# A mixer stage whose small products stand a step later, and first modulation weights in the buffers of the main inputs

## The chip, the cores and the metric

One core of a Trainium2 chip runs the whole program in one launch. The metric is the time of one execution in device microseconds; the time before is the median of three runs. TensorE (PE) multiplies, VectorE (DVE), ScalarE (ACT) and GpSimd (POOL) do the rest, and SyncE (SP) issues nearly all transfers.

## What is computed

Two transformer-like blocks follow each other on 512 tokens of width 1024; 256 context tokens go through the first block's first layer too. All is fp32. Only the first block is touched by the change. Each of its two layers is, cut to what matters:

```python
mx = split(silu(c) @ w_ada[l] + b_ada[l], 6)          # modulation, main stream
mc = split(silu(c_ctx) @ w_ada[l] + b_ada[l], 6)      # modulation, context
hx = modulate(rmsnorm(x, g), mx[0], mx[1]); hc = modulate(rmsnorm(ctx, g), mc[0], mc[1])
zx = hx @ w_in; zc = hc @ w_in
# mLSTM, 4 heads of 128, forward and backward: the context's final state starts the main stream
# gates -> running sums and maxima; scores q k^T * exp(...); states sum(w * k v^T); normalise per head
# plus a Fourier mix over 256 channels and a 31-tap depthwise convolution over 256 channels
out = concat([mlstm, fourier, conv]) @ w_out
x = x + mx[2] * rmsnorm(out); then a squared-ReLU MLP with its own modulation
```

## The kernel before

Large products run as three fp32r passes: each operand is split into a high part (a cast on ACT) and a low part (a subtraction on DVE), and lines 317 to 319 multiply high by high and the two mixed pairs. Weights come in tiles of 128x1024 (0.52 MB) through three staging buffers `st`, and `wload` (line 273 on) casts and subtracts them into four `whi` and four `wlo` buffers. Small products, those of attention and states, are plain fp32, in two passes each.

The program is written as Python code whose scheduler orders each engine's instructions by its own estimates, so the order on an engine is not the order of the source. What is hand-made is a set of side threads. A product group of the large kind (`gemm_f`, `gemm_t`) ends with `self.step(rate)`: three steps for the 512 main tokens, one for the 256 context tokens. A step resumes the next of up to three side generators to its next `yield`. So a `yield` places what follows it behind at least one more product group. The threads of a layer's `mixers` are: one per stream for the gates (`gate_thread`, line 718), one per head and stream (`head_thread` in `head`, line 847), the convolution, the Fourier mix, and a `tail` that turns and splits the finished heads. `finish` (line 306) runs out the remaining steps when the in-projections are done: there a step has no product group beside it. The finished channels lie in the tiles that held the layer's input (`new_h`), so the turning of heads waits for the last in-projection product.

In a head, `ktrans` turns the keys on PE and copies them on ACT; `kstate` scales them on ACT (line 836), a slot each, and multiplies each by the values (line 837) right behind; the sum goes into the state. The context's heads make the state, the main stream's heads use it. `short_conv` (lines 805 to 808) makes the queries and keys, `gate_thread` the gate rows, and its transposes follow two yields after their transfer.

The program opens with the first modulation. `ada_now` (line 430) loads 16 tiles of 0.52 MB through the three `st` buffers and multiplies each by the two condition vectors (line 442) on PE; columns 2 and 3 of the weight blocks first, then 0 and 1. The two context tiles are loaded and normalised meanwhile (`prenorm_a`), then modulated and split (`prenorm_b`, lines 514, 511, 313). The main inputs are loaded behind the modulation (`first_load`), get their position codes added, half on DVE, half on POOL (line 1252), and the values' weights (`win_v`) are loaded by the first `wload` of `mixers`.

Of the kernel before, what the change touches and what calls it, by code (L numbers as in the profile page):

```python
# [9 lines left out]
F32 = mybir.dt.float32  # L10
# [3 lines left out]
AF = mybir.ActivationFunctionType  # L14
OP = mybir.AluOpType

P = 128
D = 1024
T = 512
TC = 256  # L20
KT = D // P
# [9 lines left out]
NST = 3  # L31
# [195 lines left out]
class Net:  # L227
# [202 lines left out]
    def ada_now(self, w, nbs, mods):  # L430

        nc = self.nc
        n = len(mods)
        bias = self.par1[0]
        for nb in nbs:
            ps = self.psum("mm")
            for c in range(4):
                with self.tc.high_priority():
                    st = self.ws.tile([P, 1024], F32, tag="st", name=self.nm("st"), bufs=NST)
                    nc.sync.dma_start(st, w[2 * nb + c // 2][:, 1024 * (c % 2):1024 * (c % 2) + 1024])  # L440
                for k in range(2):
                    nc.tensor.matmul(ps[:n], self.cvec[:, 2 * c + k:8 * n:8], st[:, 512 * k:512 * k + 512],
                                     start=c + k == 0, stop=c + k == 4)
            row = self.slot()[:n]
            nc.vector.tensor_copy(row, ps[:n])
            ps = self.psum("s")
            for f in range(4):
                self.transpose(ps[:, n * f:n * f + n], row[:, P * f:P * f + P])
            e = slice(4 * nb, 4 * nb + 4)
            for m, mod in enumerate(mods):  # L450
                nc.vector.tensor_add(mod[:, e], ps[:, m:4 * n:n], bias[:, e])
# [273 lines left out]
    def gate_thread(self, g, li, fz, bg, t, prior, key):  # L725
        nc = self.nc
# [26 lines left out]
        nt = t // P  # L753
# [14 lines left out]
        w = li  # L768
# [7 lines left out]
        nc.sync.dma_start(dr[:, :t], M)  # L776
        yield
        yield
        ut = self.small("ut_k" if key else "ut_x", [P, 4, 2, R], bufs=1)
        wt = self.small("wt_k" if key else "wt_x", [P, 4, R], bufs=1)  # L780
        for i in range(nt):
            ps = self.psum("s")
# [10 lines left out]
        ps = self.psum("s")  # L793
# [34 lines left out]
            next(after, None)  # L828
        return v

    def kstate(self, hd, d, g, kt, v, tiles, pv):

        r = hd + 32 * d
        for n, i in enumerate(tiles):
            ks = self.slot((P, P))
            self.nc.scalar.activation(ks, kt[:, P * i:P * i + P], AF.Copy, scale=g["w"][:, i, r:r + 1])
            self.nc.tensor.matmul(pv, ks, v[:, i, hd], start=n == 0, stop=n == len(tiles) - 1)

    def ktrans(self, k, nt):
        ps = self.psum("s")  # L840
# [6 lines left out]
    def head_thread(self, hd, q, k, v, g, t, prior, new, out):  # L847


        nc = self.nc  # L850
        nt = t // P
        while not g:
            yield
        kt = self.ktrans(k, nt)
        if new is not None:
            pv = self.psum("pv")
            for d in range(2):
                self.kstate(hd, d, g, kt, v, range(nt), pv[:, 130 * d:130 * d + 130])
            nc.vector.tensor_copy(new["c"][:, hd], pv[:, :260].rearrange("p (d n) -> p d n", n=130))
            new[hd] = True  # L860
            if out is None:
                return
            yield
# [9 lines left out]
        for c in range(nch):  # L873
# [5 lines left out]
            for d in range(2):  # L879
# [19 lines left out]
                n = 0  # L899
# [8 lines left out]
        if prior is not None:  # L908
            while hd not in prior:
                yield  # L910
            states = prior["c"]
            for d in range(2):
                r = hd + 32 * d
                x = self.slot()
                for c in range(nch):
                    e = slice(256 * c, 256 * c + 256)
                    ref = g["mref"][:, 0 if (c == 0) == (d == 0) else 1, r:r + 1]
                    nc.scalar.activation(x[:, e], negm[d][:, e], AF.Exp, bias=ref)
                nc.vector.tensor_mul(x, x, q)
                qs.append(x)  # L920
            st1 = self.slot((P, 2, 130))
            pv = self.psum("pv")
            for d in range(2):
                self.kstate(hd, d, g, kt, v, (0, 1) if d == 0 else (2, 3), pv[:, 130 * d:130 * d + 130])
            for d in range(2):
                r = hd + 32 * d
                nc.vector.scalar_tensor_tensor(st1[:, d], states[:, hd, d], g["mref"][:, 2, r:r + 1],
                                               pv[:, 130 * d:130 * d + 130], op0=OP.mult, op1=OP.add)
            yield
# [179 lines left out]
    def mixers(self, l, streams, after=iter(())):  # L1109
# [6 lines left out]
        for m in streams:  # L1116
# [4 lines left out]
                whole.append(m)  # L1121
            if key:
                ctx["c"] = self.hp.tile([P, 4, 2, 130], F32, tag="cstate", name=self.nm("cstate"))
        ws = [self.wload(a["win_v"][l, c]) for c in range(2)]
        for m in streams:
            m["v"] = self.values(ws, m["h"], m["t"], "vc" if m["key"] else "vx", after)
        w = self.wload(a["win_g"][l, 0], 1024)
# [73 lines left out]
    def first_block(self):  # L1201
# [34 lines left out]
        with self.tc.high_priority():  # L1236
            xc = [self.prenorm_a(self.first_load(sc, i)[0]) for i in range(2)]
        self.ada_now(a["w_ada"], (2, 3, 0, 1), mods[0])
        xx = [self.first_load(sx, i) for i in range(4)]
        hc = self.new_h(TC, "c")  # L1240
        g = gs(0, 1, 0, "g_pre_mix")()
# [6 lines left out]
        def rest():  # L1248
            for i in range(4):
                xh, pos = xx[i]  # L1250
                for j in range(2):
                    (nc.gpsimd if j else nc.vector).tensor_add(xh[j], xh[j], pos[j])
                self.prenorm_b(self.prenorm_a(xh), i, *g, hx)
                yield
            with self.tc.issue_after(self.last_load):
# [667 lines left out]
```

## Time and profile before

| | |
|---|---|
| median of three runs | 2852.14 us (2851.42, 2852.14, 2858.28) |
| profiled execution | 2859.91 us, span of its trace 2858.1 us |
| PE busy | 2718.5 us, 95% of the span |
| DVE, ACT, POOL busy | 1686.4, 1097.8, 301.7 us |
| PE's mean granted clock | 0.973 of full |
| moved by DMA | 312.85 MB, 109 GB/s over the span |

The busy time of an engine is the union of its instructions' spans. A wait is put down to the producer that came last. The small products leave two records each in the trace, the transposes one. In the layers of the first block the mixers lie at about 60 to 380 us and 1040 to 1260 us; the opening lies ahead of them.

### The profile page before, as it was taken

The numbers are of one execution on the slowest core, as the hardware profiler recorded it, in microseconds if no ns is written. First come the engines' busy times: TensorE is split into PE (matmuls) and PEld (weight loads), VectorE is DVE, ScalarE is ACT, GpSimd is POOL, SyncE is SP. The second block draws the span as 40 slices with busy tenths as digits, with TensorE's granted clock in tenths as the row PEclk, the third lists the DMA queues.
The fourth block names the chain that finished last, engine by engine and source line by source line (L and its number), as shares of the span: only waits on it lengthen the run. The fifth ranks groups of instructions, "written<-read, shape, count | busy, mean of one in ns | idle before, by whom it ended". The sixth has DMA issues, their size and how long they took to land. (4 is left out here: it accounts for less than half of the span.)

```text
span 2858.1 us, 36796 instructions
## 1 busy us (share of the span) xinstructions
PE 2718.5 (95%) x13940; PEld 2197.9 (77%) x13940; DVE 1686.4 (59%) x3469; ACT 1097.8 (38%) x2032; POOL 301.7 (11%) x452
## 2 busy tenths in 40 slices
PE   6999998999999988998999999999999999999998
PEld 2888888888788866877888877776788777766887
DVE  3587856567734679965334467666433566674334
ACT  2543545322222364544323353445222444353222
POOL 2042001000000013201000010010012100101011
PEclk8989999999999999998999999999999999999999
DMA  7323323445612463443223332221132422111223
GB/s 271 105 84 105 106 85 108 151 132 182 230 61 67 163 200 111 133 156 132 96 81 108 106 129 89 74 75 38 46 102 89 147 76 88 53 60 41 92 89 118
DMA packets 101281, 312.85 MB, mean 109 GB/s; under 512 B 11504, under 2 KB 15368, under 8 KB 101104
## 3 DMA queue, kind: packets, MB, share of 16 engines
q1 hardware_dynamic: 100544, 309.64, 33.1%
q8 instruction: 109, 1.79, 0.3%
q0 software_dynamic: 560, 0.86, 0.1%
q14 instruction: 68, 0.56, 0.1%
HBM read 293.43 MB, written 17.03 MB: 109 GB/s over the span
## 5 line engine op out<-in xcount | busy, mean ns | idle before, releaser
L317 PE MATMUL mm<-xhi,whi 128*128 128x512 f32 (+2 forms) x1520 | 595.3, 392 | 15.8 <-DVE sl L1400 7.0
L285 DVE TENSOR_TENSOR wlo<-st,whi 128x1024 fp32r<-128x1024 f32 x352 | 441.5, 1260 | 284.6 <-ACT whi L284 279.0
L284 ACT CAST whi<-st 128x1024 fp32r<-128x1024 f32 x352 | 369.0, 1050 | 593.0 <-PE mm L318 283.4
L318 PE MATMUL mm<-xlo,whi 128*128 128x512 f32 (+2 forms) x1520 | 589.9, 388 | 0.4 <-DVE xlo L313 0.2
L319 PE MATMUL mm<-xhi,wlo 128*128 128x512 f32 (+2 forms) x1520 | 590.2, 388 | 0.0
L317 PEld LDWEIGHTS mm<-xhi,whi 128*128 128x128 f32 (+1 forms) x1520 | 289.9, 191 | 73.4 <-DVE sl L1400 7.8
L319 PEld LDWEIGHTS mm<-xhi,wlo 128*128 128x128 f32 (+1 forms) x1520 | 289.9, 191 | 56.9
L318 PEld LDWEIGHTS mm<-xlo,whi 128*128 128x128 f32 (+1 forms) x1520 | 289.7, 191 | 56.6 <-issue 1.5
L317 PE MATMUL mm<-whi,sl 128*128 128x512 f32 x640 | 250.9, 392 | 3.2 <-DVE sl L696 1.3
L319 PE MATMUL mm<-whi,sl 128*128 128x512 f32 x640 | 250.1, 391 | 1.0 <-DVE sl L313 1.0
L318 PE MATMUL mm<-wlo,sl 128*128 128x512 f32 x640 | 250.5, 391 | 0.5 <-DVE wlo L285 0.2
L317 PE MATMUL mm<-whi,xhi 128*128 128x512 f32 x576 | 229.6, 400 | 4.5 <-ACT xhi L313 4.5
L318 PE MATMUL mm<-wlo,xhi 128*128 128x512 f32 x576 | 228.8, 397 | 0.2
L319 PE MATMUL mm<-whi,xlo 128*128 128x512 f32 x576 | 227.8, 396 | 0.6 <-DVE xlo L313 0.4
L352 PE MATMUL s<-ident,sl 128*128 128x128 f32 (+2 forms) x756 | 123.5, 284 | 63.4 <-ACT sl L511 15.2
L352 PEld LDWEIGHTS s<-ident,sl 128*128 128x128 f32 (+2 forms) x756 | 87.6, 144 | 115.3 <-issue 34.4
L383 DVE CUSTOM_DVE_ANT_0 sa<-sa,crow 128x1024 f32<-128x1024 f32 x112 | 137.0, 1225 | 40.5 <-DMA sa<-in_w_ada 27.4
L317 PEld LDWEIGHTS mm<-whi,sl 128*128 128x128 f32 x640 | 120.6, 188 | 30.6 <-DVE sl L696 1.9
L319 PEld LDWEIGHTS mm<-whi,sl 128*128 128x128 f32 x640 | 120.6, 188 | 26.7 <-DVE sl L313 1.8
L318 PEld LDWEIGHTS mm<-wlo,sl 128*128 128x128 f32 x640 | 120.6, 188 | 26.6 <-DVE wlo L285 2.1
L313 ACT CAST sl<-sl 128x512 fp32r<-128x512 f32 (+2 forms) x144 | 70.6, 500 | 171.9 <-DVE sl L650 129.4
L317 PE MATMUL mm<-chi,whi 128*128 128x256 f32 (+1 forms) x448 | 134.6, 301 | 1.1 <-ACT chi L313 1.1
(372 smaller groups left out, 4372.4 us busy)
## 6 DMA issues: line engine op xcount, KB each, us to landing
st<-in_w_mlp SPq DMA_DIRECT2D x128, 512.0 KB
st<-in_win_a SPq DMA_DIRECT2D x116, 512.0 KB
sa<-in_w_ada SPq DMA_DIRECT2D x80, 512.0 KB
sa<-in_ada SPq DMA_DIRECT2D x48, 512.0 KB
st<-in_win_b SPq DMA_DIRECT2D x40, 512.0 KB
st<-in_w_out SPq DMA_DIRECT2D x32, 512.0 KB
xres<-sl SPq DMA_DIRECT2D x48, 256.0 KB
sl<-xres SPq DMA_DIRECT2D x48, 256.0 KB
```

Source lines behind the costliest of these rows:

```text
L284: nc.scalar.copy(hi, st)
L285: nc.vector.tensor_sub(lo, st, hi.bitcast(F32))
L313: return self.nc.scalar.copy(hi, src), self.nc.vector.tensor_sub(lo, src, hi.bitcast(F32))
L317: mm(ps, l[0], r[0], start=first, stop=False)
L318: mm(ps, l[0], r[1], start=False, stop=False)
L319: self.last_mm = mm(ps, l[1], r[0], start=False, stop=last).ins
L352: self.nc.tensor.transpose(out, src, self.ident[:p, :p])
L383: nc.vector.tensor_tensor_reduce(x, st[:, e], row[:, e], 1.0, 0.0, op0=OP.mult, op1=OP.add, accum_out=part[:, m, f, h:h + 1])
```

## The change

It has three parts. The first modulation's weights go into the two tiles that later hold the main stream's split input (`xhi` and `xlo`, tags of the pool `hx`): four loads to a tile, alternating, with all eight products of a block behind them in the source, and the value weights are then loaded at once behind the last of these loads, ahead of the main inputs. The four additions of position codes that POOL did go to DVE. And the threads have more yields: one in the gates ahead of their transposes; one at the start of a head; one in context heads behind the key transposes; and one inside `kstate` between the scaled copies, which now go into one slot, and the products with the values.

```diff
         for b, nb in enumerate(nbs):
             ps = self.psum("mm")
-            for c in range(4):
-                with self.tc.high_priority():
-                    st = self.ws.tile([P, 1024], F32, tag="st", name=self.nm("st"), bufs=NST)
-                    nc.sync.dma_start(st, w[2 * nb + c // 2][:, 1024 * (c % 2):1024 * (c % 2) + 1024])
-                for k in range(2):
-                    nc.tensor.matmul(ps[:n], self.cvec[:, 2 * c + k:8 * n:8], st[:, 512 * k:512 * k + 512],
-                                     start=c + k == 0, stop=c + k == 4)
+            with self.tc.high_priority():
+                st = self.hx.tile([P, KT, T], F32, tag="xlo" if b % 2 else "xhi", name=self.nm("ada"))
+                for c in range(4):
+                    self.last_load = nc.sync.dma_start(
+                        st[:, 2 * c:2 * c + 2],
+                        w[2 * nb + c // 2][:, 1024 * (c % 2):1024 * (c % 2) + 1024].rearrange("p (k n) -> p k n", n=T)).ins
+            for k in range(8):
+                nc.tensor.matmul(ps[:n], self.cvec[:, k:8 * n:8], st[:, k], start=k == 0, stop=k == 7)
...
         nc.sync.dma_start(dr[:, :t], M)
         yield
         yield
+        yield
...
-    def kstate(self, hd, d, g, kt, v, tiles, pv):
-        r = hd + 32 * d
-        for n, i in enumerate(tiles):
-            ks = self.slot((P, P))
-            self.nc.scalar.activation(ks, kt[:, P * i:P * i + P], AF.Copy, scale=g["w"][:, i, r:r + 1])
-            self.nc.tensor.matmul(pv, ks, v[:, i, hd], start=n == 0, stop=n == len(tiles) - 1)
+    def kstate(self, hd, g, kt, v, tiles):
+        ks = self.slot()
+        parts = [(d, n, i) for d in range(2) for n, i in enumerate(tiles[d])]
+        for x, (d, n, i) in enumerate(parts):
+            r = hd + 32 * d
+            self.nc.scalar.activation(ks[:, P * x:P * x + P], kt[:, P * i:P * i + P], AF.Copy,
+                                      scale=g["w"][:, i, r:r + 1])
+        yield
+        pv = self.psum("pv")
+        for x, (d, n, i) in enumerate(parts):
+            self.nc.tensor.matmul(pv[:, 130 * d:130 * d + 130], ks[:, P * x:P * x + P], v[:, i, hd], start=n == 0,
+                                  stop=n == len(tiles[d]) - 1)
+        return pv
...
         nt = t // P
+        yield
         while not g:
             yield
         kt = self.ktrans(k, nt)
         if new is not None:
-            pv = self.psum("pv")
-            for d in range(2):
-                self.kstate(hd, d, g, kt, v, range(nt), pv[:, 130 * d:130 * d + 130])
+            yield
+            pv = yield from self.kstate(hd, g, kt, v, [range(nt)] * 2)
...
-            pv = self.psum("pv")
-            for d in range(2):
-                self.kstate(hd, d, g, kt, v, (0, 1) if d == 0 else (2, 3), pv[:, 130 * d:130 * d + 130])
+            pv = yield from self.kstate(hd, g, kt, v, [(0, 1), (2, 3)])
...
-        ws = [self.wload(a["win_v"][l, c]) for c in range(2)]
+        ws = [self.wload(a["win_v"][l, c]) for c in range(2)] if l else self.first
...
         self.ada_now(a["w_ada"], (2, 3, 0, 1), mods[0])
+        with self.tc.issue_after(self.last_load):
+            self.first = [self.wload(a["win_v"][0, c]) for c in range(2)]
...
-                    (nc.gpsimd if j else nc.vector).tensor_add(xh[j], xh[j], pos[j])
+                    nc.vector.tensor_add(xh[j], xh[j], pos[j])
```

The diff does not tell where the scheduler then puts things. Three places show it. The names are tile names with a running number.

SP's queue in the opening, before: `st` are staging buffers, `sl` context tiles, `sa` weights of later modulations, and PE in a wait is the consumer of the buffer's former content.

```order
L409 DMA sa_681<-in_w_ada 128x1024
L440 DMA st_161<-in_w_ada 128x1024 [waits DMAHW1_49,PE_49]
L440 DMA st_175<-in_w_ada 128x1024 [waits DMAHW2_49,DMAHW0_49,PE_49]
L440 DMA st_179<-in_w_ada 128x1024 [waits DMAHW3_49,PE_49]
L552 DMA sl_132<-in_ctx 128x512
L440 DMA st_183<-in_w_ada 128x1024 [waits DMAHW7_49,PE_49]
L440 DMA st_187<-in_w_ada 128x1024 [waits DMAHW4_49,DMAHW0_49,PE_49]
L440 DMA st_201<-in_w_ada 128x1024 [waits DMAHW5_49,DMAHW1_49,PE_49]
L552 DMA sl_133<-in_ctx 128x512 [waits DMAHW6_49]
L440 DMA st_205<-in_w_ada 128x1024 [waits DMAHW3_49,PE_49]
L440 DMA st_209<-in_w_ada 128x1024 [waits DMAHW4_49,PE_49]
L440 DMA st_213<-in_w_ada 128x1024 [waits DMAHW5_49,PE_49]
```

The same stretch of the changed program, from the third context tile to the first value weight; line 441 is the new load.

```order
L554 DMA sl_132<-in_ctx 128x512 [waits DMAHW2_49]
L554 DMA sl_133<-in_ctx 128x512 [waits DMAHW3_49]
L409 DMA sa_667<-in_w_ada 128x1024 [waits DMAHW4_49]
L441 DMA ada_195<-in_w_ada 128x1024 [waits DMAHW5_49,DMAHW6_49,DMAHW0_49,PE_49]
L441 DMA ada_195<-in_w_ada 128x1024
L441 DMA ada_195<-in_w_ada 128x1024 [waits DMAHW7_49]
L441 DMA ada_218<-in_w_ada 128x1024 [waits DMAHW1_49,PE_49]
L441 DMA ada_218<-in_w_ada 128x1024
L441 DMA ada_218<-in_w_ada 128x1024 [waits DMAHW2_49]
L441 DMA ada_195<-in_w_ada 128x1024 [waits DMAHW3_49]
L441 DMA ada_218<-in_w_ada 128x1024 [waits DMAHW4_49]
L283 DMA st_240<-in_win_v 128x1024 [waits DMAHW5_49]
```

The loads of the second pair of blocks wait for PE twice, at the first of each tile, and the value weights follow directly; the main inputs come behind six more transfers.

PE's queue in layer 1's mixers, first context head, before: line 352 turns the keys, 317 to 319 are in-projection products, 837 multiplies scaled keys by values.

```order
L352 MATMUL s_9452<-ident,sl_9372 128x128 x2
L317 MATMUL mm_9494<-xhi,whi_9359 128x512
L318 MATMUL mm_9494<-xlo,whi_9359 128x512
L319 MATMUL mm_9494<-xhi,wlo_9360 128x512
L317 MATMUL mm_9494<-xhi,whi_9359 128x512
L837 MATMUL pv_9457<-vc_8805,sl_9458 128x130
L318 MATMUL mm_9494<-xlo,whi_9359 128x512
L837 MATMUL pv_9457<-vc_8805,sl_9461 128x130
L837 MATMUL pv_9457<-vc_8805,sl_9464 128x130
L837 MATMUL pv_9457<-vc_8805,sl_9467 128x130
```

The same products in the changed program, where line 845 has taken the place of 837; the turning of the keys stands 48 in-projection products ahead of these rows.

```order
L317 MATMUL mm_9501<-chi,whi_9495 128x256
L318 MATMUL mm_9501<-clo,whi_9495 128x256
L319 MATMUL mm_9501<-chi,wlo_9496 128x256
L845 MATMUL pv_9526<-vc_8769,sl_9469 128x130 x4
L317 MATMUL mm_9537<-xhi,whi_9489 128x512
L318 MATMUL mm_9537<-xlo,whi_9489 128x512
L319 MATMUL mm_9537<-xhi,wlo_9490 128x512
```

The four state products stand together, 48 products behind the transposes in place of four.

PE's queue in layer 1 behind the last in-projection product, before: line 944 multiplies probabilities and states by values and queries, 994 is the Fourier mix.

```order
L319 MATMUL mm_10717<-xhi,wlo_10632 128x512
L944 MATMUL pv_10742<-vx_8859,sl_10501 128x130
L944 MATMUL pv_10742<-cstate_8776,sl_10677 128x130
L944 MATMUL pv_10742<-vx_8859,sl_10501 128x130 x2
L944 MATMUL pv_10742<-cstate_8776,sl_10677 128x130
L944 MATMUL pv_10754<-vx_8859,sl_10585 128x130 x2
L944 MATMUL pv_10754<-cstate_8776,sl_10681 128x130
L944 MATMUL pv_10754<-vx_8859,sl_10585 128x130
L944 MATMUL pv_10754<-cstate_8776,sl_10681 128x130
L994 MATMUL s_10766<-sl_10661,sl_10518 128x257
L994 MATMUL s_10766<-sl_10665,sl_10523 128x257
```

The changed program behind its last in-projection product: 887 is the former 877 (scores), 986 the former 978 (Fourier, first half), 352 turns the last two heads' keys.

```order
L319 MATMUL mm_10368<-xhi,wlo_10308 128x512
L352 MATMUL s_10393<-ident,sl_9694 128x128 x4
L887 MATMUL s_10404<-sl_9693,sl_9694 128x256 x2
L352 MATMUL s_10421<-ident,sl_9821 128x128 x2
L887 MATMUL s_10485<-sl_9693,sl_9694 128x256 x2
L986 MATMUL s_10508<-cs_110,sl_10017 128x256
L986 MATMUL s_10508<-cs_110,sl_10018 128x256
L845 MATMUL pv_10502<-vc_8769,sl_10480 128x130 x4
L986 MATMUL s_10513<-cs_110,sl_10017 128x256
L986 MATMUL s_10513<-cs_110,sl_10018 128x256
L352 MATMUL s_10532<-ident,sl_9861 128x128 x4
L887 MATMUL s_10543<-sl_9860,sl_9861 128x256 x2
```

Here two heads still have their scores and states to make when the in-projections are over. Counted to the first product of the output projection, 40 small instructions stand there before, 92 now; at the same place of layer 0, between the last in-projection product and the first output product, 76 and 134. On DVE the work that belongs to these stretches is 154 instructions in layer 0 and 100 in layer 1.

## Rows read from the trace of the kernel before

**Rows 1.** busy time of the engines: us, share, weight loads beside, from the page

```profile
PE 2718.5 (95%) x13940; PEld 2197.9 (77%) x13940; DVE 1686.4 (59%) x3469; ACT 1097.8 (38%) x2032; POOL 301.7 (11%) x452
```

**Rows 2.** PE waits of the whole span: us in total, times, longest

```profile
PE mm L442 <- DMA st<-in_w_ada: 13.8, 6, 7.0
```

**Rows 3.** windows: busy (x records) PE, PEld, DVE, ACT, POOL; clock, DMA share, GB/s

```profile
0.00:20.00 20.00, 10.53 (x18) 1.78 (x19) 1.64 (x6) 4.28 (x9) 6.46 (x20) 0.91 0.78 277
6.00:10.00 4.00, 3.04 (x5) 0.53 (x6) 0.35 (x2) 0.83 (x3) 0.79 (x5) 1.00 1.00 361
10.00:14.00 4.00, 3.57 (x9) 0.57 (x7) 0.26 (x1) 0.99 (x3) 0.94 (x3) 1.00 1.02 392
```

**Rows 4.** timeline of the opening: start, us, engine, instruction, idle before

```profile
45.58 1.88 PE L442 MATMUL mm<-st,cvec 128*2 128x512 f32 x4 [0.68 <-DMA st<-in_w_ada]
...
49.86 0.15 DVE L451 TENSOR_TENSOR mod0c<-s,par 128x4 f32<-128x4 f32 x1
...
52.32 1.14 ACT L313 CAST chi<-sl 128x512 fp32r<-128x512 f32 x2
...
57.59 2.93 ACT L284 CAST whi<-st 128x1024 fp32r<-128x1024 f32 x3
...
59.75 5.64 DVE L285 TENSOR_TENSOR wlo<-st,whi 128x1024 fp32r<-128x1024 f32 x3
...
62.10 0.79 PE L318 MATMUL mm<-wlo,chi 128*128 128x512 f32 x1 [2.19 <-DVE wlo L285]
...
68.47 1.21 DVE L285 TENSOR_TENSOR wlo<-st,whi 128x1024 fp32r<-128x1024 f32 x1
```

**Rows 5.** PE waits from 60 to 450 us, layer 0

```profile
PE pv L944 <- DVE sl L919: 1.7, 1, 1.7
PE s L352 <- DVE sl L901: 1.6, 1, 1.6
PE s L352 <- DVE sl L751: 1.6, 1, 1.6
```

**Rows 6.** PE waits from 1000 to 1100 us, gates of layer 1

```profile
PE s L352 <- DVE sl L751: 2.3, 2, 2.0
```

**Rows 7.** PE waits from 1100 to 1300 us, heads of layer 1

```profile
PE s L352 <- DVE sl L808: 4.3, 3, 3.0
PE mm L317 <- DVE sl L808: 3.6, 1, 3.6
...
PE pv L837 <- ACT sl L836: 2.8, 2, 2.1
```

**Rows 8.** windows in the mixers, columns as in rows 3

```profile
350.00:380.00 30.00, 27.09 (x179) 23.74 (x178) 23.78 (x90) 21.70 (x58) 1.52 (x2) 1.00 0.38 115
1200.00:1270.00 70.00, 65.56 (x337) 55.50 (x336) 54.45 (x154) 30.21 (x68) 4.83 (x3) 0.95 0.56 181
250.00:260.00 10.00, 10.00 (x67) 10.00 (x66) 6.24 (x16) 1.88 (x7) 0.00 (x0) 0.73 0.32 103
1120.00:1130.00 10.00, 5.96 (x18) 4.47 (x18) 10.00 (x8) 0.00 (x0) 9.57 (x6) 0.83 0.47 157
```

**Rows 9.** PE timeline at the ends of both in-projections

```profile
346.72 0.60 PE L352 MATMUL s<-ident,sl 128*128 128x128 f32 x4
...
353.49 1.89 PE L978 MATMUL s<-cs,sl 128*128 128x256 f32 x8
...
377.20 0.48 PE L317 MATMUL mm<-whi,chi 128*128 128x512 f32 x1
...
1248.68 0.38 PE L944 MATMUL pv<-vx,sl 128*128 128x130 f32 x2
...
1257.84 0.48 PE L317 MATMUL mm<-whi,xhi 128*128 128x512 f32 x1
1258.15 0.39 PE L318 MATMUL mm<-wlo,xhi 128*128 128x512 f32 x1
1258.38 0.40 PE L319 MATMUL mm<-whi,xlo 128*128 128x512 f32 x1
```

More of the change, by code (lines that the diff above doesn't have):

```diff
@@ L434, in ada_now @@
         bias = self.par1[0]
-        for nb in nbs:
+        for b, nb in enumerate(nbs):
             ps = self.psum("mm")
-            for c in range(4):
-                with self.tc.high_priority():
-                    st = self.ws.tile([P, 1024], F32, tag="st", name=self.nm("st"), bufs=NST)
-                    nc.sync.dma_start(st, w[2 * nb + c // 2][:, 1024 * (c % 2):1024 * (c % 2) + 1024])
-                for k in range(2):
-                    nc.tensor.matmul(ps[:n], self.cvec[:, 2 * c + k:8 * n:8], st[:, 512 * k:512 * k + 512],
-                                     start=c + k == 0, stop=c + k == 4)
+            with self.tc.high_priority():
[6 more added lines that the diff above has]
+                nc.tensor.matmul(ps[:n], self.cvec[:, k:8 * n:8], st[:, k], start=k == 0, stop=k == 7)
             row = self.slot()[:n]
```

## Prediction

> **What bounds the kernel now.** I read the page's busy shares first. TensorE (PE) is busy for 2718.5 of 2858.1 us [rows 1], far more than any other engine. So PE's queue is the bound, and a change that leaves its products alone can only take from the 139.6 us in which PE is idle, or from stretches in which its clock is granted below full. I then asked where that idle time lies that the change can reach: the opening, and the two mixer stages (about 60 to 450 us and 1040 to 1270 us). Outside these the two orders of PE are the same, product for product.
>
> In the opening PE waits 13.8 us for the first modulation weights [rows 2]. The timeline shows why the stage is long: the last of these products runs at 45.58, the context's modulation is done at 49.86, its first normalised half is cast from 52.32. But the first value weights are only cast from 57.59, their low parts take until 65.4, and PE streams from 62.10 [rows 4]. The windows show that the transfers were not saturated: two 4 us windows move 361 and 392 GB/s, the first 20 us only 277 on average [rows 3].
>
> In the mixers PE waits for a few named producers. Layer 0: 1.7, 1.6 and 1.6 us [rows 5]. Layer 1: 2.3 us at the gates [rows 6], 4.3 and 3.6 us for the short convolution, 2.8 us for the scaled keys [rows 7]. In layer 1 these fall in a stretch in which DVE has no idle time: 10.00 of 10 us [rows 8].
>
> **The opening.** The three shared buffers are replaced by two large ones that hold four tiles each. The first eight loads now need no buffer to come free; in the first order excerpt two waits on PE stand where nine stood. Up to the last modulation tile the queue now carries 4 context tiles of 0.26 MB, 16 modulation tiles of 0.52 MB and one later-modulation tile: 10.0 MB. At 370 GB/s, between the two saturated windows [rows 3], that is 27 us from the first movement at about 3 us, and I allow 1 for the constants that POOL loads beside it: 31 us, where the trace has 45.58 [rows 4]. Four value tiles and one more later-modulation tile, 2.6 MB, take 7 us more: 38 us. The fourth needs the first one's buffer, and then its cast and its subtraction (1.21 us where POOL is idle [rows 4]): 41 us. The context's normalisation stands behind these in DVE's and ACT's queues, so it starts then and not at 49.86. From 49.86 the first half was ready at about 53.4 (two casts of 1.14 us from 52.32), so 3.5 us: PE's first product at about 45 us instead of 62.10, a gain of 17. The main inputs are now issued behind weight tiles on SP that wait for DVE, and land around 52 us (1.6 MB of weights and 3.4 MB of inputs are 13.5 us from 38); they are wanted only after the context's 48 value products. The low end: if the transfers keep the old mean of 277 GB/s, the modulation ends at 41, the value tiles at 50, the first product falls at 56, and the gain is 6. I take 13, nearer the saturated rows because the SP rows shown lose nearly all their waits on PE.
>
> The Trainium skill, DMA: Bandwidth & Descriptors, Specifications, puts the limit of one core's HBM at about 358 GB/s. The rows show 361 and 392, so this run exceeds it; by the page's figure the modulation would end 1 us later, and the sum would be 1 us less.
>
> The four additions that move from POOL to DVE cost DVE 4 x 0.7 us, and free the subtractions: three took 5.64 us beside POOL, 1.88 each, against 1.21 alone [rows 4]. I count this as nothing; DVE has time while PE does the context's products.
>
> **The lag, where it gains.** One yield more puts a step, up to 24 large products (0.23 us apart [rows 9], 5.5 us), between the transposes, the scaled copies and the small products. In the second order excerpt 48 products stand where four stood, so the 2.8 us go, and likewise the gate's 2.3 us and the key transposes' 4.3. The 3.6 us is PE waiting for a PSUM bank that a saturated DVE has not emptied; with heads later, DVE is freer there, and I expect most of it to go. Of 13.0 us in layer 1 I take 10, bounds 0 (DVE stays saturated) and 15 with the clock of that stretch (0.83 of full in a window [rows 8], 1.7 us). In layer 0 4.9 us go; one wait of 1.7 us is followed by a window at 0.73 [rows 8], 2.7 us lost there, so I take 7, bounds 0 and 10.
>
> **The lag, where it costs.** Every context head takes three steps more, every head of the main stream two, each gate one: 4 x 3 + 4 x 2 + 2 = 22 steps a stage. Steps run three to a large product group, one to a context group; what is left when the in-projections end runs in `finish` with no product beside it. The third order excerpt shows it. In layer 1 PE had 40 small instructions between the last in-projection product and the first output product; now 92. In layer 0: 76, now 134. Before, these uncovered stretches lasted 23.7 us (353.49 to 377.20) and 9.2 us (1248.68 to 1257.84) [rows 9].
>
> Their price, by engine. A small fp32 product leaves two records, a transpose one. In the window 350 to 380 us PE had 179 records in 27.09 us, 0.151 each, and DVE 90 instructions in 23.78 us, 0.264 each, at 79% busy [rows 8]. Layer 0: PE's 118 products and 16 transposes are 252 records, 38 us; DVE's 154 instructions of that stretch are 41 us at full, 51 at 79%. So PE waits 3 to 13 us there, against 1.7 before (146 records, 22.0 us, in 23.7). I take 6 more; bounds 1 and 11. Layer 1: 166 records, 25 us; DVE's 100 instructions are 35 us by that stage's 0.354 each (54.45 us for 154 [rows 8]), 45 at 78% busy, so PE waits 10 to 20 us, less what output products on the finished channels cover (27 stand early, 0.23 each, 6 us). I take 10; bounds 4 and 20.
>
> **Sum.** -13 - 7 + 6 - 10 + 10 = -14 us. The profiled execution took 2859.9 us, 7.8 above the median of the three runs, 2852.1; the sum gives 2845.9 for it, and 2838 for a median. A measurement here can tell about 0.3%, 8.6 us, from no change.
>
> **Rivals.** *The tails run one head behind the other* (slower). In the finishing rotation a head's chain is transposes, copy, scores, exponentials, states, sums, norm. One head of layer 0 took from 346.72 to about 377 us [rows 9], 30 us. If the last head finds nobody to hide it, each tail is PE's own 38 or 25 us plus some 29. Waits of 58, 56 more than before in place of 16, give -14 + 40 = +26: 2878. It decides from tail waits of about 39 us in all. For it: three heads stand in layer 0's tail, two in layer 1's. Against: the order interleaves them, with Fourier products between. Chance 0.11.
>
> *The opening yields 6 and the mixers nothing*: -6 - 3 - 5 + 14 = 0: 2852. For it: DVE is saturated in layer 1, and its work is only moved. Chance 0.14.
>
> *The clock falls in the tails.* A wait of 1.7 us was followed by 0.73 of full, a mix of the 1.2 and 2.4 GHz levels [rows 5, 8]; but 350 to 380, with its waits, stayed at 1.00 [rows 8]. If both tails (63 us of PE work) ran at 0.73 they would lose 17 us: +3, 2855. Chance 0.08. The Trainium skill, TensorE: Matmul & The Clock Gate, HAM oscillation, says that waits between bursts bring the half clock back each time; by that rule this rival holds, and the window 350 to 380 speaks against it.
>
> *The tails hide too* (their waits at the low bounds, 1 and 4 more): -13 - 7 - 10 + 5 = -25: 2827. For it: output products stand among the last small ones. Chance 0.17.
>
> **How the numbers follow.** My forecast has 0.50: 2838, alone within 2828 to 2848. Faster by over 0.3% collects it and the last rival: 0.67. Within: 0.14 + 0.08 = 0.22. Slower: 0.11. The range 2822 to 2856 takes in all but the slower rival and the outer ends of the bounds.
>
> **What the profile after would show.** First in-projection product at 45 to 50 us, no wait of PE for value weights, DMA share near 1 in the first 40 us. No wait of PE on scaled keys; little on the short convolution. Uncovered stretches of about 45 and 35 us at the ends of both in-projections, with new waits on DVE and ACT. I am wrong if the first product comes after 55 us, if those stretches last over 55 us each, or if the clock in them is below 0.8.

## The result, and the profile after

The change is slower: median 2872.59 us of six runs (2868.12 to 2880.01) against 2857.65 of six runs of the kernel before beside them (2851.42 to 2866.34). The ratio is 1.0066, with a 95% interval of 1.0049 to 1.0084, some 19 us by that ratio (the medians differ by 14.9). The profiled execution took 2868.12 us, its span is 2866.4; that is only 8.3 more than the span of before, since the change's profiled execution is the fastest of its six and that of before lay high among its runs. Below, prices come from ratios of timed runs (0.001 is 2.85 us), and traces say where the time lies.

The page after, busy times of the engines; it answers to [rows 1]. PE is busy as long as before:

```profile
PE 2717.5 (95%) x13940; PEld 2198.1 (77%) x13940; DVE 1689.5 (59%) x3473; ACT 1098.5 (38%) x2032; POOL 293.5 (10%) x448
```

The opening after: PE's waits from 0 to 60 us, then windows (busy and records of PE, PEld, DVE, ACT, POOL; clock, DMA share, GB/s), then rows of PE's timeline:

```profile
PE mm L445 <- DMA ada<-in_w_ada: 9.4, 1, 9.4
PE s L352 <- ACT sl L513: 3.1, 1, 3.1
```

```profile
0.00:20.00 20.00, 10.48 (x19) 1.69 (x20) 1.02 (x5) 3.63 (x8) 6.49 (x20) 1.00 0.88 312
10.00:14.00 4.00, 3.88 (x6) 0.44 (x5) 0.00 (x0) 0.00 (x0) 0.00 (x0) 1.00 1.02 390
20.00:40.00 20.00, 20.00 (x57) 4.37 (x55) 4.61 (x13) 4.12 (x7) 0.95 (x3) 1.00 0.85 309
```

```profile
27.59 10.46 PE L445 MATMUL mm<-ada,cvec 128*2 128x512 f32 x24
...
48.35 0.50 PE L317 MATMUL mm<-whi,chi 128*128 128x512 f32 x1 [0.20 <-ACT chi L313]
```

PE's first in-projection product stands at 48.35 instead of 62.10 [rows 4]; the first 20 us move 312 GB/s instead of 277 [rows 3], and six waits for the first weights have become one [rows 2]. From 20 to 40 us PE itself is full with the modulation, and the DMA share is 0.85: once the first loads have landed, the 64 modulation products keep PE busy from 9.40 to 41.06 us with hardly a pause.

PE's waits in the mixers after: 60 to 450 us, 1000 to 1100, and 1100 to 1300; they answer to [rows 5 to 7]:

```profile
PE pv L845 <- ACT sl L840: 5.3, 2, 5.0
PE pv L952 <- DVE sl L911: 3.9, 2, 2.8
PE s L352 <- DVE sl L911: 2.9, 2, 1.6
PE s L402 <- DMA sa<-in_w_ada: 2.2, 1, 2.2
PE pv L845 <- ACT sl L961: 2.1, 1, 2.1
```

```profile
PE s L352 <- DVE wt_k L789: 4.4, 1, 4.4
```

```profile
PE pv L845 <- ACT sl L840: 9.3, 2, 7.8
PE pv L952 <- DVE sl L935: 3.9, 1, 3.9
PE pv L952 <- ACT sl L961: 3.5, 1, 3.5
PE s L352 <- DVE sl L811: 2.9, 1, 2.9
```

L845 (the states' products) waits for L840 (the scaled copies) as L837 did for L836 before, but 9.3 us instead of 2.8 [rows 7]; the gates' wait is 4.4 instead of 2.3 and names another producer, `wt_k`, DVE's copies of the turned gates out of PSUM [rows 6]. The short convolution's two waits, 7.9 us, are 2.9.

Windows after, as [rows 8], and below them the two uncovered stretches:

```profile
350.00:380.00 30.00, 22.75 (x135) 20.23 (x134) 22.13 (x96) 16.31 (x46) 2.01 (x4) 0.89 0.17 47
250.00:260.00 10.00, 10.00 (x70) 9.25 (x69) 9.89 (x25) 7.80 (x21) 1.23 (x1) 1.00 0.32 105
1120.00:1130.00 10.00, 10.00 (x51) 8.43 (x50) 10.00 (x16) 3.21 (x5) 3.21 (x3) 1.00 0.16 53
1200.00:1270.00 70.00, 55.13 (x303) 46.69 (x301) 51.72 (x155) 31.62 (x81) 2.63 (x2) 0.90 0.52 163
```

```profile
316.00:376.00 60.00, 42.59 (x249) 37.79 (x248) 40.23 (x164) 30.53 (x91) 3.53 (x5) 0.83 0.24 75
1223.00:1266.00 43.00, 29.75 (x160) 25.32 (x159) 31.56 (x106) 19.09 (x51) 1.35 (x2) 0.84 0.47 145
```

PE's timeline after, at the ends of both in-projections, as [rows 9]:

```profile
315.32 0.39 PE L319 MATMUL mm<-xhi,wlo 128*128 128x512 f32 x1
...
332.97 1.07 PE L952 MATMUL pv<-vx,sl 128*128 128x130 f32 x4
...
339.90 0.61 PE L952 MATMUL pv<-vx,sl 128*128 128x130 f32 x4
...
362.36 2.10 PE L845 MATMUL pv<-vx,sl 128*128 128x130 f32 x8 [5.05 <-ACT sl L840]
...
376.24 0.47 PE L317 MATMUL mm<-whi,chi 128*128 128x512 f32 x1
...
1266.29 0.48 PE L317 MATMUL mm<-whi,xhi 128*128 128x512 f32 x1
```

Layer 0's in-projections end 38 us earlier than before, at 315.32, and the first output product still stands where it stood, 376.24 against 377.20. The whole gain is gone in a stretch of 61 us. In its window PE is busy for 42.6 us of 60 and no engine is full (DVE 40.2): PE waits by turns for ACT and DVE. The clock falls beside it: four records of small products that take 0.61 us at 339.90 take 1.07 at 332.97.

### The profile page after: what moved, and what is told of

It is laid out like the page before. It is cut to its first block, busy times and chain, and to the rows that moved or that the text cites. A ratio compares the mean times of both kernels' runs of the same rounds, so it can differ in the third digit from the quotient of the medians.

```text
span 2866.4 us, 36807 instructions
## 1 busy us (share of the span) xinstructions
PE 2717.5 (95%) x13940; PEld 2198.1 (77%) x13940; DVE 1689.5 (59%) x3473; ACT 1098.5 (38%) x2032; POOL 293.5 (10%) x448
## 5 line engine op out<-in xcount | busy, mean ns | idle before, releaser
L352 PEld LDWEIGHTS s<-ident,sl 128*128 128x128 f32 (+2 forms) x756 | 87.8, 143 | 118.7 <-issue 30.7
```

Of the source, the lines that this page charges most:

```text
L352: self.nc.tensor.transpose(out, src, self.ident[:p, :p])
```

## The experiments

The theory: the opening gains 13 us; the lag's extra steps lose more than they gain, since what is left over at the end of the in-projections runs there as chains of small products.

**The two halves.** The first kernel has the opening with the mixers of before, the second the reverse.

```diff
 # the opening alone: functions of the mixers as before
-        yield                       (gate_thread, head_thread, kstate)
 # the lag alone: ada_now and first_block as before
-        ws = [...] if l else self.first
+        ws = [self.wload(a["win_v"][l, c]) for c in range(2)]
```

> Only the opening of the change (large buffers for the first modulation weights, the first value weights asked for early, the four additions on DVE); the mixers' threads as before. Theory (the opening gains, the extra steps lose it in the uncovered stretches at the ends of the in-projections): the 13 us stay, ratio 0.995 to 0.996, first in-projection product near 48 us, uncovered stretch of layer 0 about 24 us again (76 small PE instructions), of layer 1 about 9 us (40). Rival (the opening's gain is given back inside layer 0 by itself, for the later main inputs or DVE's four additions): ratio 0.998 to 1.000, with new waits between 60 and 350 us.

> Only the lag of the change (one step more for the gates, for each head's start, for the context's states and for the scaled copies, which lie in one slot); the opening as before. Theory: the extra steps gain some 17 us of waits and lose some 40 in the two uncovered stretches, +23 us, ratio 1.007 to 1.009, stretches of about 60 and 44 us. Rival (the lag and the early opening only hurt together, since the threads run nearer to their inputs): ratio 0.998 to 1.003.

Measured: the opening alone 0.9954 (0.9939 to 0.9970), 13 us gained. The lag alone 1.0107 (1.0091 to 1.0124), 30 us lost, more than the 23 expected. Their sum, 1.0061, is the change's 1.0066: they do not work on each other, and both rivals fall. The opening's stretches, in windows:

```profile
334.00:358.00 24.00, 21.27 (x143) 19.32 (x142) 17.36 (x66) 15.88 (x48) 1.01 (x1) 0.93 0.36 117
1230.00:1238.00 8.00, 8.00 (x59) 7.57 (x59) 6.66 (x15) 3.94 (x11) 0.00 (x0) 1.00 0.83 274
```

With the opening alone on one side and the change on the other, the lag can be booked stretch by stretch. PE's own records that moved are priced at 0.151 us [rows 8]: into the uncovered stretches 249 - 143 = 106 in layer 0 and 160 - 59 = 101 in layer 1. Layer 1's in-projections lost 20 more, which run behind the first output product (opening alone above, change below):

```profile
999.51:1229.47 229.96, 208.77 (x1045) 171.70 (x1044) 199.96 (x442) 121.88 (x251) 49.32 (x49) 0.96 0.45 146
1016.57:1222.19 205.62, 187.95 (x924) 155.16 (x922) 177.41 (x351) 104.69 (x206) 43.79 (x47) 0.95 0.46 149
```

| stretch, from PE's timelines, us | opening alone | change | price of records moved | lag's share |
|---|---|---|---|---|
| layer 0, in-projections | 48.74 to 333.00: 284.3 | 48.35 to 315.32: 267.0 | -16.0 | -1.3 |
| layer 0, uncovered | to 358.09: 25.1 | to 376.24: 60.9 | +16.0 | +19.8 |
| layer 1, in-projections | 999.51 to 1229.47: 230.0 | 1016.57 to 1222.19: 205.6 | -18.3 | -6.1 |
| layer 1, uncovered | to 1238.86: 9.4 | to 1266.29: 44.1 | +15.3 | +19.4 |

The sum is 31.8 us; without the 3.0 of the records that run later it is 28.8, and the two spans differ by 28.1. How finely single traces can be booked is seen where nothing differs: up to 264 us the order of PE, DVE and ACT is the same, record for record, in the opening alone and in the control with four late steps (below), and the control's trace takes 7.1 us longer for it. So the in-projections' shares lie within what two executions can differ by, the uncovered stretches' far outside.

**The steps one by one.** Five kernels share the opening; the first has the scaled copies in one slot and no extra step, the others add steps.

```diff
 e6: -yield after "negm", -yield at a head's start, -yield ahead of the context's states, -yield in kstate
 e11: e6 + the gates' yield            e10: e6 + the yield ahead of the context's states
 e3: e10 + the yield in kstate         (the change: e3 + the gates' yield + the heads' start)
```

> The change without any of its extra steps: the opening, and the scaled copies of the keys of both directions in one slot, all copies ahead of the first small product. 76 and 40 small PE instructions are left over, as before. Theory (the extra steps lose the time): as the opening alone, ratio 0.994 to 0.997. Rival (the one slot makes PE wait for the last of the copies): 0.998 to 1.003, with waits of PE for the copies of 2 us and more at each head.

> The opening, the scaled copies in one slot, and of the extra steps only the gates' one. Nothing more is left over (76 and 40). Theory: as the opening alone or 2 to 4 us below it (PE's waits for the gates' rows, 1.6 us in layer 0 and 2 to 3.6 in layer 1, go), ratio 0.993 to 0.996. Rival (a gate one step later holds up every head behind it, and DVE's copy of the gates' transposes becomes the wait, as in the change): 0.997 to 1.000.

> The opening, the scaled copies in one slot, and of the extra steps only the one between a context head's transposes and its states (80 and 52 small PE instructions left over). Theory (each small instruction left over costs about 0.6 us of uncovered stretch and gives 0.3 back before it): 4 and 12 more than the opening alone, some 5 us, ratio 0.995 to 0.9985. Rival (any lag of the contexts holds up the main stream's heads, which wait for their states): 0.999 to 1.003.

> The change without the extra step of the gates and without the extra step at each head's start; the steps for the context's states and for the scaled copies stay. The order then has 110 small PE instructions in layer 0's uncovered stretch and 80 in layer 1's (the change 134 and 92, before 76 and 40). Theory (loss by the steps that are left over): the loss of 21 and 19 us shrinks with them to about 12 and 15, which with the gains of 13 and 15 gives 0 us against before, ratio 0.998 to 1.002. Rival (the scaled copies in one slot, four copies ahead of the first small product, are what costs): as the change, 1.004 to 1.008.

| kernel | small PE instructions left over | uncovered stretches, us | ratio (95%) |
|---|---|---|---|
| e6, no extra step | 76, 40 | 23.9, 9.4 | 0.9947 (0.9928 to 0.9967) |
| e11, gates | 76, 40 | 23.9, 9.4 | 0.9987 (0.9971 to 1.0003) |
| e10, contexts' states | 80, 52 | 31.1, 18.1 | 0.9973 (0.9959 to 0.9987) |
| e3, and the scaled copies | 110, 80 | 42.3, 31.1 | 1.0030 (1.0020 to 1.0040) |
| the change | 134, 92 | 60.9, 44.1 | 1.0066 (1.0049 to 1.0084) |

The one slot costs nothing, so that rival falls. The context's step costs 7 us against e6 and 5 against the opening alone, as the theory had it, though the intervals overlap. The step behind the scaled copies, the one that the change is named after, costs 16, and the last row, the gates' step and the heads' start together, adds 10. The stretches grow with what is left over, by (60.9 - 23.9) / (134 - 76) = 0.64 us for one more instruction in layer 0 and (44.1 - 9.4) / (92 - 40) = 0.67 in layer 1, while before it gives back two records, 0.30. That is the mean of a chain, not a price for each: e3's stretches give 0.54, and the four more of e10 in layer 0 cost 7.2 us. e3 came out slower than expected (0.998 to 1.002).

The gates' step was a miss: it costs 11 us with nothing more left over. Its trace shows that the wait it was meant for does not go. PE's waits from 1000 to 1100 us, with the step and without:

```profile
PE s L352 <- DVE wt_k L789: 5.6, 1, 5.6
```

```profile
PE s L352 <- DVE sl L753: 4.0, 2, 3.6
```

One step later the operand is there, and PE waits instead until DVE has emptied the PSUM bank. That is 1.6 us more. Windows of layer 0, with the step and without, show a difference in the clock:

```profile
220.00:230.00 10.00, 7.58 (x40) 6.55 (x38) 9.72 (x17) 5.28 (x13) 0.68 (x1) 0.85 0.20 69
230.00:240.00 10.00, 10.00 (x48) 10.00 (x49) 1.60 (x6) 2.63 (x8) 0.00 (x0) 0.50 0.24 90
```

```profile
220.00:230.00 10.00, 8.29 (x60) 7.51 (x60) 8.50 (x19) 6.65 (x16) 0.00 (x0) 1.00 0.29 96
230.00:240.00 10.00, 10.00 (x63) 10.00 (x62) 4.98 (x13) 1.20 (x5) 0.00 (x0) 0.66 0.34 115
```

With the step PE runs ten microseconds at half clock. Over 100 to 260 us the clock costs 20.8 us with it and 12.0 without (one less the clock, over four windows of 40 us), and at the first output product of layer 1 the kernel with the step is 9.2 us behind (1245.04 against 1235.82). That is not much more than the 7.1 us by which two traces of one order differed above, so the 11 us are not accounted for.

**Is it latency?** The whole change, with `finish` running one thread to its end after the other.

```diff
 def finish(self, *gens):
+    wide, self.wide = self.wide, 1
     while any(g in self.side for g in gens):
         self.step()
+    self.wide = wide
```

> The whole change, but what is left over at the end of the in-projections runs one thread to its end after the other, instead of three in turn. The same instructions, 126 small PE ones in layer 0's uncovered stretch and 104 in layer 1's. Theory (there PE waits for the chain from step to step within a head): with nothing between a head's steps the stretches grow by a third or more, to 80 us and over and to 58 us and over, ratio 1.014 to 1.030. Rival (PE is slow in small products there, or its clock is low, whatever their order): stretches of about 57 and 50 us, ratio 1.005 to 1.009.

Measured: 1.0158 (1.0131 to 1.0185), 26 us more than the change; the ratio is the theory's, but the stretches, 65.3 and 54.7 us, fall between the two and nearer to the rival. Some 6 us lie behind layer 1: `finish` serves the second network's stages too. Windows of the stretches:

```profile
317.00:381.00 64.00, 44.84 (x238) 37.02 (x237) 41.36 (x177) 28.25 (x87) 4.53 (x6) 0.79 0.23 68
1230.00:1284.00 54.00, 35.26 (x183) 29.94 (x182) 37.50 (x131) 20.95 (x58) 3.33 (x3) 0.78 0.35 116
```

No engine is full here either. In layer 1 twelve more small instructions are left over, which at 0.67 us each are 8 of the 10.6 us. In layer 0 the stretch is 4 us longer although eight fewer are left over, which at 0.64 us are 5 more: turns of three save 4 to 10 us of 65. So this run does not prove that it is latency; that rests on PE's waits in the stretches and on the next runs. That the change's heads all but follow one another already would explain the small effect, but is not shown.

**Giving the left-over steps a cover.** The whole change with more steps to each of the last six product groups of a stage: five, or eight. Then the same on the opening alone, with four, as a control.

```diff
+        self.rate = 5               # or 8; the control: 4
         w = self.wload(a["win_a"][l, 6])
...
+        self.rate = RATE1
         for m in whole:
             m["y"] = self.new_h(m["t"], m["st"]["kind"])
```

> The whole change, but the last six product groups of each mixer stage (Fourier inputs and gates of the output) take five steps each instead of three (two instead of one to a context group). The order up to there is the change's own; 74 and 50 small PE instructions are left over, like before's 76 and 40. Theory (what is left over costs, 20 us in layer 0 and 19 in layer 1): both fall by two thirds or more, ratio 0.992 to 0.997. Rival (the lag costs wherever its steps run, since the heads' chains follow one another): little changes, ratio 1.001 to 1.006, and waits of PE move in among the last six groups.

> The whole change, with eight steps instead of three to each of the last six product groups of a mixer stage (four instead of one to a context group); no stretch with more than 32 small PE instructions is left. At five steps the loss was halved, with 74 and 50 left over. If what is left over is itself the cost, this goes further: ratio 0.993 to 0.999. If the pace is what counts (steps that come faster than the engines behind them make their operands, with or without products beside them), it comes back: ratio 1.001 to 1.006, with more waits of PE among the last six groups.

> The opening alone (mixers as before), with four steps instead of three to the last six product groups of each mixer stage: no uncovered stretch of 30 or more small PE instructions is left in either stage. It could beat both kernels. Theory (small instructions cost more where no product lies beside them: 25 us for 76 of them in layer 0): a further 5 to 10 us below the opening alone, ratio 0.992 to 0.994. Rival (PE has its own work in that stretch and is only busy elsewhere instead): as the opening alone, 0.9955.

Measured: five steps 1.0002 (0.9990 to 1.0015), eight 0.9972 (0.9958 to 0.9987), the control 0.9992 (0.9974 to 1.0009). Eight steps give back 27 of the change's 32 us over the opening. Windows with eight, over the ends of both in-projections, and PE's waits from 315 to 377 us:

```profile
290.00:376.00 86.00, 78.54 (x475) 68.44 (x474) 63.74 (x245) 39.98 (x108) 5.84 (x7) 0.98 0.25 78
1190.00:1247.00 57.00, 53.83 (x304) 46.42 (x303) 47.19 (x153) 27.60 (x73) 2.01 (x2) 0.97 0.56 180
```

```profile
PE pv L952 <- ACT sl L961: 0.7, 1, 0.7
PE pv L845 <- ACT sl L840: 0.6, 1, 0.6
PE pv L952 <- DVE den L955: 0.2, 1, 0.2
```

The same small products beside large ones leave PE 1.5 us of waits from 315 us on, and 7.5 without work in the whole window at a clock of 0.98; the change has 17.4 and 0.88 in the same window. So most of the loss is shown to come from steps that are left without cover. Five steps fell between theory and rival: 74 and 50 are as few as before, and the stretches are 29.6 and 20.7 us, not 24 and 9, since what is left are the ends of late heads. The control was a miss: it is 11 us slower than the opening alone. That covering those 76 and 40 is what costs is not shown: in its trace 7.1 us are lost ahead of the point where the orders part, at a lower clock (0.91 against 0.94 from 49 to 230 us).

**The pace of the whole stage.** Four steps to a group instead of three, everywhere, with the lag and without.

```diff
-RATE1, WIDE1 = 3, 3
+RATE1, WIDE1 = 4, 3
```

> The change with four steps to a large product group in the first network's mixers instead of three, and two instead of one to a context group. Nothing else differs; 42 small PE instructions are then left over in layer 0 and 52 in layer 1. Theory (the loss is what is left over): the loss in layer 0 goes and that in layer 1 shrinks to some 5 us; with the gains of 13 and 17 the time falls to about 20 us below before, ratio 0.991 to 0.995. Rival (DVE's work in the mixers is the bound and the tail only shows it): the waits move into the in-projections, the time stays at the change's or between it and before, ratio 0.999 to 1.006.

> The opening alone (mixers as before) with four steps to a large product group and two to a context group: the other half of the pair with the change at four steps, which came out 10 us slower than before although only 42 and 52 small PE instructions were left over. No uncovered stretch has more than 32 small PE instructions here. If the faster rate itself costs (small products, and with them clock falls, are packed into the first half of the stage), this run loses much of the opening's 13 us: ratio 0.998 to 1.003. If the lag costs wherever its steps run, the rate is harmless here: ratio 0.990 to 0.9955.

Measured: 1.0034 (1.0022 to 1.0047) with the lag and 1.0116 (1.0092 to 1.0140) without. The first came out where its rival had it. The second went far beyond what was expected: the pace itself costs the opening's kernel 46 us. In the traces PE is idle for 31 us more and busy for 24 more with the same 13940 records, at a mean clock of 0.967 instead of 0.978; the profiled execution lay 10 us above its median. PE's waits from 1100 to 1300 us, with the lag and without:

```profile
PE mm L317 <- DVE sl L811: 7.9, 1, 7.9
PE s L352 <- DVE sl L811: 5.1, 1, 5.1
```

```profile
PE s L352 <- DVE sl L810: 19.5, 4, 7.8
PE mm L317 <- DVE sl L810: 6.4, 1, 6.4
```

At this pace PE waits 25.9 us for DVE in the short convolution and the lag halves it; by the ratios the lag gains 23 us there. At three steps these waits were 7.9 us [rows 7], and there was little to gain.

**What stayed open.** Eight late steps without the gates' step, then without the heads' start too.

```diff
 e13: e12 - the gates' yield        e14: e13 - the yield at a head's start
```

> The change without the gates' step, with eight steps instead of three to each of the last six product groups; at most 35 small PE instructions left over in a stretch. Theory (the loss has two parts, what is left over and the gates' step, 10 us each way measured alone): 0.9972 less the gates' 0.0036, ratio 0.992 to 0.995, level with the opening alone or better. Rival (the gates' step costs only where the heads behind it stay as before): no change against the run with the gates' step, 0.996 to 0.999.

> As the run before, and without the steps at the heads' starts too: only the contexts' step and the one behind the scaled copies stay; at most 30 small PE instructions left over. Theory (a step at a head's start moves the whole head and separates no operand from its product, so it neither gains nor loses once nothing is left over): the same ratio within 0.002. Rival (later heads give DVE time in the crowded stretch of layer 1, so the start's steps gain there): 0.002 to 0.004 slower than with them.

Measured: 0.9972 (0.9961 to 0.9984) and 0.9997 (0.9985 to 1.0009). The gates' step costs nothing here, so its 11 us depend on the order around it; why stays open. The heads' later start gains 7 us once nothing is left over: both times the rival had the ratio. Whether DVE's time is the reason, as the rival says, is not shown.

**The additions.** The opening alone, half of the additions on POOL again.

```diff
-                    nc.vector.tensor_add(xh[j], xh[j], pos[j])
+                    (nc.gpsimd if j else nc.vector).tensor_add(xh[j], xh[j], pos[j])
```

> The opening alone, but with half of the position additions on POOL again, as before the change. The prediction counted their move to DVE as nothing. If so: as the opening alone, ratio 0.994 to 0.997. If the move is what lets the subtractions of the first weights run unhindered: some 2 to 5 us slower than the opening alone, 0.997 to 0.999.

Measured: 0.9975 (0.9964 to 0.9987), against the opening's 0.9954: the move is worth about 6 us, though the two intervals overlap slightly. PE's wait for the first normalised main tile from 46 to 100 us, with the additions on POOL and without:

```profile
PE s L352 <- ACT sl L498: 4.7, 1, 4.7
```

```profile
PE s L352 <- ACT sl L498: 1.0, 1, 1.0
```

POOL's timeline with them shows what holds it up: POOL also makes the root by which a tile is normalised, and that stands behind all four additions, each of which waits for its input. Below it two of the additions on DVE in the opening alone.

```profile
54.19 1.70 POOL L1256 TENSOR_TENSOR sl<-sl,sl 128x512 f32<-128x512 f32 x1 [32.16 <-DMA sl<-in_k_pos]
...
60.21 1.26 POOL L1256 TENSOR_TENSOR sl<-sl,sl 128x512 f32<-128x512 f32 x1 [0.69 <-DMA sl<-in_x]
...
61.98 0.55 POOL L347 TENSOR_TENSOR rq_y<-ms,mhalf 128x1 f32<-128x1 f32 x1
```

```profile
53.05 1.29 DVE L1256 TENSOR_TENSOR sl<-sl,sl 128x512 f32<-128x512 f32 x2
```

The kernel that beats both is the opening alone, 13 us below before; with one slot for the copies, 15, which is the same within the intervals.

## Why the prediction was wrong

**The opening, -13: right in sum, wrong in its parts.** Measured -13. PE started at 48.35, not 45: the sum took the transfers as the only bound of the modulation, at 370 GB/s. They ran at 312, and PE's own 64 products, which the sum left out, took until 41.06 instead of 31. Of the 13 us some 6 are, by that run, the four additions, which the prediction counted "as nothing; DVE has time": DVE had, but POOL's queue was not followed to the root behind them. The Trainium skill, GPSIMD Engine Reference, Engine selection, advises VectorE for such additions since GpSimd takes about twice as long; the rows agree, 1.26 to 1.70 us on POOL against 1.29 for two on DVE in the opening's kernel, but here the place in the queue cost more than the duration.

**The lag's gain in layer 0, -7: wrong, -1.** The three waits of [rows 5] went, and a wait for modulation weights (2.2 us, of DMA) and two small ones took their place. The clock costs 12 us both in the change and in the opening alone (one less the clock, over four windows of 40 us from 100 to 260): without the waits it fell as often, so the 2.7 us that the prediction put down to a wait of 1.7 did not come back.

**The lag's gain in layer 1, -10: right in direction, some -6.** PE was without work for 21.2 us of the in-projections in the opening alone and for 17.7 in the change, only 3.5 less. The short convolution's waits fell by 5.0, as forecast. The gates' 2.3 us became 4.4: the prediction took the wait for one on an operand; one step later it is one on the bank. And PE's products with probabilities and states got new waits, 3.5 us until ACT has emptied a bank (L961) and 1.5 for DVE's copy of the state.

**The tails, +6 and +10: here it failed.** "I take 6 more" and "I take 10" were 20 and 19. The step that failed is the division of a stretch by the busiest engine: 41 to 51 us of DVE were set against 38 of PE and the difference taken as PE's waiting. DVE was busy 40.2 us in layer 0's stretch, just as forecast, and PE waited 17.4 us (60 - 42.6) all the same, for ACT and DVE in turn: in a head each step needs the one before, and few heads are left. In layer 1 it waited 13.3, within the bounds of 4 and 20. PE's own work also took 42.6 and 29.8 us instead of 38 and 25, at a clock of 0.83 and 0.84, which the sum had at nothing. With the measured parts the sum is -13 - 1 - 6 + 20 + 19 = +19, as timed; that it fits so closely is luck, given what two traces can differ by.

The rival *The tails run one head behind the other* gave 2878 and had 0.11; it decides from "about 39 us in all". PE's waits in both stretches are 17.4 + 13.3 = 30.7, short of that, and only the clock's 4.6 + 4.8 bring the loss to 40; so neither the forecast nor this rival held as written. It was put low because "the order interleaves them"; by the one-thread run that is worth 4 to 10 us in layer 0. The rival *The clock falls in the tails* came with it, with 9 us; its own 17 is too low for its 0.73, since 63 us of work take 23 longer at that clock. The Trainium skill, TensorE: Matmul & The Clock Gate, HAM oscillation, would have had it so, and the stretch of 0.83 now agrees; the window at 1.00 that spoke against it was one in which PE waited 2.9 us of 30.

The marks set for the profile after: the first product at 45 to 50, met; stretches of 45 and 35, measured 61 and 44, so "over 55 us each" came true in layer 0 alone; a clock below 0.8 there, not met (0.83 and 0.84); "No wait of PE on scaled keys", missed: the two longest waits of the tails, 5.0 and 7.8 us, are on them.

## What to carry to other kernels

A step of lag that is added to every thread is paid at the end of the stage, where nothing is left to cover it: count the steps that are left over, and price them from a stretch that already runs without cover, not at the busy time of the fullest engine. Whether a step of lag takes a wait away or moves it has to be measured step by step: here it took 5.0 of 7.9 us from the short convolution and made the gates' 2.3 into 4.4. Lag and pace work on each other: with the lag, four steps to a group or eight at the end were better than three (1.0034 and 0.9972 against 1.0066); without it, three were best (0.9954 against 0.9992 and 1.0116).

## What the runs showed of the hardware that was not expected

PE's granted clock stood at 0.50, its lower level, through ten microseconds in which PE was busy all the time (230 to 240 us with the gates' step), after 2.4 us without work; and at 0.66 in the same place after 1.7. It is tempting to put this down to the wait. The change with eight late steps speaks against it: PE has no wait at all from 190 to 250 us there, and the clock falls all the same, behind two blocks of sixteen modulation products of 128x2 (L402).

```profile
220.00:230.00 10.00, 10.00 (x67) 9.63 (x66) 8.36 (x19) 5.05 (x9) 3.85 (x3) 0.80 0.48 165
230.00:240.00 10.00, 10.00 (x47) 9.86 (x47) 1.56 (x10) 2.15 (x4) 2.45 (x2) 0.51 0.39 151
```

```profile
222.14 1.84 PE L402 MATMUL s<-cvec,sa 128*128 128x2 f32 x16
```

Such blocks also stand between the wait and the fall in the trace of before (245.54 and 247.45 us). So an engine that is busy all the time can lose half its clock; whether these products, the waits or both bring it about, no run here separates.

A kernel that packs the same products more densely, four steps to a group, lost 46 us with the same instructions. And kernels whose order is the same up to there differed by 6 to 7 us over the first 250 to 264, with the clock as the visible difference (0.91 against 0.94 in one pair, 0.90 against 0.94 in the other, five late steps and eight).
